# Hybrid conv/RWKV-7 block: the last LayerNorm in the first phase, BK times KR in quarters, squares in two parts, and a refitted planner clock

## The chip, the cores and the metric

The kernel runs on one core of a Trainium2 chip. The metric is the device time of one execution in microseconds, median over runs of one program. The engines are TensorE (PE; PEld is its weight load), VectorE (DVE), ScalarE (ACT), GpSimd (POOL) and SyncE (SP, which here issues the transfers).

## The reference

Sequence 2048, width 1024, one layer. The input is normalised and modulated, then projected once to 9344 columns, which feed two branches; both are gated, projected, merged and projected again.

```python
h = _rmsnorm(x, norm_g[l]) * (1.0 + scale[:, None, :]) + shift[:, None, :]
p = jnp.einsum('bsd,de->bse', h, w_in[l])
# conv branch
u = val * jax.nn.sigmoid(gate)
u = _causal_depthwise_conv(u, conv_k, conv_b)      # 31 taps per channel
u = _layernorm(u, ln_g, ln_b, LN_EPS)              # over the 1024 channels
y_conv = (jax.nn.silu(u) * jax.nn.silu(og)) @ w_o
# rwkv branch: token shift, then per head of 64
kk = (k * k_k); kk = kk / max(sqrt(sum(kk * kk)), L2_EPS)
state = state * w_t - (state @ kk_t) (kk_t * a_t) + v_t k_t     # a scan over time
y_rwkv = (groupnorm(o) + bonus) * jax.nn.silu(og) @ w_o
# merge
m = sigmoid(g_conv) * y_conv + sigmoid(g_rwkv) * y_rwkv
x = x + gate * (m @ w_out);  out = _rmsnorm(x, final_g)
```

## The kernel before

**Layout.** Channels lie on partitions, time on the free axis. Time is cut into 4 blocks b of 512 steps (`NB`, `TB`), channels into 8 tiles j of 128 (`KT`). Products in full accuracy are made from two fp32r parts: `hi` is the value cast to fp32r (ACT), `lo` the value minus `hi` (DVE or POOL), and three products hi*hi, hi*lo, lo*hi are summed in PSUM (`mm3k`, L347). A projection is 24 such matmuls of 512 columns.

**First phase** (`manual_schedule`, from L1425). For each block, four groups g of 18 projections each. The projections k, r, vv of the two pairs of a group (a pair q is two heads, 128 channels) feed `pair` (L755); the others are the convolution's gate and value ("c") and the four gates "1" to "4" (`order`, L1358, with the lists `FILL` and, for the last group, `LAST`). Results that are needed later go to DRAM scratch: `y_dram` (after the 31 taps), `co_dram`, `ro_dram`, `gr_dram`, `gc_dram` (gates), `z_dram` (rwkv branch before its projection), `u_dram` (conv branch before its projection). The phase ends with `rows0` (L1456): both branch projections of block 0, "ro" then "co".

**Order by a model clock.** Every engine call goes through `note` (L85), which keeps a modelled time for each engine (`RATE`, constants for SP and PE) and for each tile. Work beside the projections is written as Python generators, `Task`s with a rank (0 first); `poll` (L152) emits their next instructions when the model says that what they wait for (`ok`, `idle`, `room`, `bank`, `burst`) is there. So the constants in `note` decide in which order instructions stand in each engine's queue. On the chip each engine takes its queue in order; an instruction put too early blocks those behind it.

**What the change touches in `pair`.** The squares of k (`sq`, ACT) are summed over the 64 channels of each head by a product with `bones`, a block matrix of ones, in plain fp32 (L806 to L808); the sums go to `ssr` and to DRAM (`G.dN`), where the group's chain reads them. Then `y` and `BK` are made, and L841 to L855 multiply `BK` by `KR` for each chunk of 64 steps: for each head `hh` 64 contraction rows, 128 output partitions, 128 columns, into one of two PSUM banks `pA`; DVE masks the result into `Asb`. One burst is 8 such products (16 records, since fp32 takes two each); a pair has two bursts.

**LayerNorm.** For blocks 0 to 2 it is `lnorm_first` (L1189), part of the side tasks of the next block (`sides`, L1323, rank 3, one after the other, from group 1 on): pass 1 loads the 8 tiles of y and sums them (POOL), a product with `ones` gives the mean; pass 2 loads them again, subtracts, squares (ACT), sums; a second product gives the variance and `rsteps` (L273) the inverse root on DVE in ten steps; pass 3 loads y a third time, subtracts and multiplies on POOL, applies swish (ACT, DVE), multiplies by the gate and stores to `u_dram`. Buffers are `hx` (L503), a ring of 7 tiles shared with the input norm (`xnorm`), the group's end (`zb`, `zr`), `hload` (which fetches the next block's input) and `presplit` (L305). `presplit` writes the hi and lo parts of the 8 `w_ro` and 8 `w_o` tiles to DRAM, in two halves each; `sides` places four in block 1, four in block 2 and eight in block 3.

For block 3 the norm is `lnorm` (L1566) in the second phase, with y kept in 8 tiles of pool `b2` and two PSUM tiles `pmean`, `pvar`.

**Convolution.** `conv` (L1144) makes `u`; `taps` (L1170, rank 4) adds the 31 taps on DVE into a PSUM tile and stores y. There are three `u` tiles, and a `u` waits for the convolution three before it.

**Second phase** (from L1601, ordered by the tile framework's own scheduler). For each block b: `cproj` of the conv branch (b > 0), loads and splits of the next block's z and u (`lsplit`, through 6 `ld` buffers), the output product (`part`, 384 matmuls of 256 columns, PSUM tiles `pout`), the residual sum and squares (`addx`), the final norm (`tail_rs`, `finish`), and `rproj` of the next block, whose results `mr` share buffers with the stored outputs `xt`.

## Time and profile before

| | us |
|---|---|
| median of 3 runs (lowest, highest) | 2893.17 (2893.12, 2894.62) |
| the profiled execution, its own time | 2892.82 |
| its span, first to last instruction | 2890.7 |

The page gives each engine's busy share, 40 slices, and the costliest groups. All rows name L129, the line of the wrapper through which every call goes, so groups are told apart by tile names (`out<-in`). In a timeline row stand start, duration, engine, operation, tiles, shape and count, and in brackets the idle time before it and what ended it. PE durations overlap (matmuls are pipelined): the distance of two starts is what a matmul costs.

### The profile page before, as it was taken

The page shows a single profiled execution, that of the slowest core. Times are in us where ns is not written, and L with a number is a line of the kernel's source. Part 1 is how long each engine was busy: PE and PEld are TensorE (multiplying, and loading weights), DVE is VectorE, ACT ScalarE, POOL GpSimd, SP SyncE. Part 2 cuts the span into 40 slices and gives each one's busy share as a digit, 9 for nine tenths or more (in the row PEclk, how much of TensorE's full clock was granted, in tenths as well). Part 3 has the DMA queues.
Part 4 walks back from the last instruction along what each step waited for, and adds up shares of the span by engine and source line. Part 5 has one row for each costly group of instructions (what it writes and reads, how often), then busy time and mean ns, then how long its engine had stood idle before and what let it go on. Part 6 is the DMA issues. An engine that isn't in the chain of part 4 may idle for free.

```text
span 2890.7 us, 52304 instructions
## 1 busy us (share of the span) xinstructions
PE 2725.4 (94%) x19472; PEld 2201.6 (76%) x19472; DVE 2058.8 (71%) x3575; ACT 1090.7 (38%) x2180; POOL 1257.7 (44%) x1772
## 2 busy tenths in 40 slices
PE   6999999889999999999999999999999998899998
PEld 5777777667777777787777777777777777698988
DVE  6877787869677878885868787669787666543343
ACT  5545344434243434443434443333434233221211
POOL 0564746533528355444656462648373633100000
PEclk9999999989999999999999999999999999999999
DMA  8786767666757566776756686866666848676665
GB/s 329 255 295 219 281 221 263 237 227 234 231 187 257 183 218 237 250 258 221 252 181 233 205 294 201 273 211 215 205 246 213 294 158 314 234 240 229 215 226 175
DMA packets 361742, 680.47 MB, mean 235 GB/s; under 512 B 134160, under 2 KB 152912, under 8 KB 361488
## 3 DMA queue, kind: packets, MB, share of 16 engines
q1 hardware_dynamic: 361488, 677.13, 69.0%
q8 instruction: 154, 2.52, 0.4%
q14 instruction: 100, 0.82, 0.1%
HBM read 494.34 MB, written 181.54 MB: 234 GB/s over the span
## 4 chain that ended last, share of the span: by engine, by line
PE 32%; DVE 9%; POOL 7%; DMA 5%; issue 3%; ACT 1%; SPq 1%; DVEq 0%; POOLq 0%; ACTq 0%
PE ps_main L129 21%; PE pout L129 5%; DVE acc L129 3%; PE xo L129 2%; PE aux L129 2%; POOL TT L129 2%; POOL itmp L129 1%; PE late L129 1%; SPq L129 1%; DVE S L129 1%; DMA w_lo<-kl_in 1%; POOL oc L129 1%; DVE gst L129 1%; DVE rs_t L129 1%; POOL lny L129 1%
## 5 line engine op out<-in xcount | busy, mean ns | idle before, releaser
L129 PE MATMUL ps_main<-h_hi,w_hi 128*128 128x512 f32 x2432 | 1016.7, 418 | 17.4 <-DVE lora L129 4.6
L129 PE MATMUL ps_main<-h_hi,w_lo 128*128 128x512 f32 x2432 | 967.7, 398 | 20.3 <-POOL w_lo L129 13.6
L129 PE MATMUL ps_main<-h_lo,w_hi 128*128 128x512 f32 x2432 | 963.8, 396 | 2.0 <-DVE h_lo L129 2.0
L129 DVE SCALAR_TENSOR_TENSOR acc<-u,ck,acc 128x512 f32<-128x512 f32 x928 | 697.5, 752 | 25.3
L129 PEld LDWEIGHTS ps_main<-h_hi,w_lo 128*128 128x128 f32 x2432 | 463.4, 191 | 130.7 <-POOL w_lo L129 16.8
L129 PEld LDWEIGHTS ps_main<-h_hi,w_hi 128*128 128x128 f32 x2432 | 464.0, 191 | 128.9 <-issue 10.0
L129 PEld LDWEIGHTS ps_main<-h_lo,w_hi 128*128 128x128 f32 x2432 | 464.9, 191 | 99.8 <-issue 7.8
L129 POOL TENSOR_TENSOR w_lo<-w_st,w_hi 128x1024 fp32r<-128x1024 f32 (+1 forms) x83 | 165.2, 1990 | 302.9 <-ACT w_hi L129 248.7
L129 POOL TENSOR_TENSOR TT<-TT,itmp 128x126 f32<-128x126 f32 (+22 forms) x496 | 207.3, 418 | 38.9
L129 ACT ACTIVATE th<-ps_main 128x512 f32<-128x512 f32 x160 | 95.6, 598 | 333.9 <-PE ps_main L129 281.7
L129 ACT CAST w_hi<-w_st 128x1024 fp32r<-128x1024 f32 (+1 forms) x135 | 127.2, 943 | 243.2 <-DMA w_st<-w_co_t 137.3
L129 POOL TENSOR_TENSOR itmp<-La,TT 128x126 f32<-128x126 f32 (+22 forms) x496 | 200.8, 405 | 37.1 <-issue 6.4
L129 DVE SCALAR_TENSOR_TENSOR S<-xo,pe,Se 64x64 f32<-64x64 f32 x512 | 145.0, 283 | 90.1 <-PE xo L129 65.3
L129 ACT COPY uv<-xo 64x256 f32<-64x256 f32 (+1 forms) x192 | 81.0, 438 | 238.3 <-PE xo L129 164.7
L129 POOL TENSOR_TENSOR lny<-lny 128x512 f32<-128x512 f32 x90 | 119.9, 1340 | 108.9 <-DMA lny<-y_d 87.0
L129 DVE TENSOR_TENSOR w_lo<-w_st,w_hi 128x1024 fp32r<-128x1024 f32 x52 | 72.4, 1392 | 68.3 <-PE ps_main L129 46.5
L129 ACT ACTIVATE Se<-S,pe 128x128 f32<-128x128 f32 x256 | 88.7, 396 | 83.2 <-DVE S L129 82.7
L129 DVE TENSOR_TENSOR As<-aux,maskA 128x512 f32<-128x512 f32 x128 | 82.3, 685 | 52.5 <-PE aux L129 52.5
L129 POOL TENSOR_TENSOR wlo<-wf,wl 64x128 fp32r<-64x128 f32 x64 | 31.2, 488 | 149.6 <-ACT wl L129 147.0
L129 ACT ACTIVATE t<-ps_main,mu 128x512 f32<-128x512 f32 x96 | 65.9, 687 | 77.6 <-PE ps_main L129 68.0
L129 DVE TENSOR_TENSOR xt<-pout,xt 128x256 f32<-128x256 f32 x64 | 24.4, 419 | 99.3 <-PE pout L129 93.2
L129 PEld LDWEIGHTS xo<-S,KR 128*128 128x128 f32 x512 | 76.8, 189 | 23.9 <-DVE S L129 5.3
(298 smaller groups left out, 5029.0 us busy)
## 6 DMA issues: line engine op xcount, KB each, us to landing
w_hi<-kh_in SPq DMA_DIRECT2D x219, 512.0 KB
w_lo<-kl_in SPq DMA_DIRECT2D x219, 512.0 KB
w_st<-w_in_t SPq DMA_DIRECT2D x73, 512.0 KB
kh_in<-w_hi SPq DMA_DIRECT2D x71, 512.0 KB
kl_in<-w_lo SPq DMA_DIRECT2D x71, 512.0 KB
lny<-y_d SPq DMA_DIRECT2D x72, 256.0 KB
w_hi<-kh_ro SPq DMA_DIRECT2D x32, 512.0 KB
w_lo<-kl_ro SPq DMA_DIRECT2D x32, 512.0 KB
```

Of the source, the lines that this page charges most:

```text
L129: r = f(*a, **k)
```

## The change

Five edits. (1) `note`: SP 0.45 us instead of 0.36 an issue, ACT 0.1 us more per further operand, scans at twice the rate per element, `scalar_tensor_tensor` of 64 columns 0.08 us more. (2) `sq` is split into two fp32r parts, and two fp32r products replace the plain one. (3) Each product of BK and KR is cut into two of 64 output partitions, so that one burst is 16 products (32 records) of 64x64. (4) `lnorm` and its pools go; `last_norm` runs `lnorm_first` for block 3 as a second task of rank 3, with the adding and multiplying on DVE, once the last convolution is done, in buffers of its own (`Slots`: the three `u` tiles and `yj`, three lent from `hx` after the norm of block 2, three more when the pairs are done). In all four norms, pass 2 squares into a tile of its own and stores y minus mean back to `y_dram`, so that pass 3 subtracts no more. (5) The order around it: block 3 has its convolutions in groups 0 to 2 (`LAST`), the norm of block 2 begins in group 0 of block 3, `presplit`s stand eight in block 1 and eight in block 2, `ld` has 8 buffers, and in the second phase the loads of x come ahead of the split of z, that of u behind the residual sums.

```diff
@@ -42,9 +42,12 @@
 WB = 6
+LDB = 8
+SLACK = 2.0
 KEPT = ("in",)
 FILL = ("c", "1", "3", "4", "2", "c", "1", "3", "4", "2")
-LAST = ("c", "1", "c", "3", "4", "2", "1", "3", "4", "2")
+LAST = ("c0 10 20 c1 21 11 22 c2 23", "c3 12 24 c4 25 13 26 c5 27", "c6 14 30 c7 31 15 32 33 34 35",
+        "16 36 37 40 41 17 42 43 44 45 46 47")
 DMA_RATE = 330e3
@@ -107,12 +110,19 @@
         elif name == "SP":
-            vt["SP"] = t + 0.36
+            vt["SP"] = t + 0.45
             vt["DMA"] = max(vt["DMA"], t) + size(out) * out.shape[0] * 4 / DMA_RATE
             c0, c1_ = RATE[name] if op != "memset" else (0.1, 0.9e-3)
-            end = vt[name] = t + c0 + c1_ * max([size(out)] + [size(a) for a in ins[:1]])
+            n_ = max([size(out)] + [size(a) for a in ins[:1]])
+            if name == "ACT":
+                c0 += 0.1 * max(len(ins) - 1, 0)
+            elif op == "tensor_tensor_scan":
+                c1_ *= 2
+            elif name == "DVE" and op == "scalar_tensor_tensor" and n_ == CH:
+                c0 += 0.08
+            end = vt[name] = t + c0 + c1_ * n_
         ready[k_] = max(ready.get(k_, 0.0), end)
@@ -235,6 +245,25 @@
                 self.free.append(max(ready.get(key(t), 0.0), used.get(key(t), 0.0)))
+
+    class Slots(Ring):
+
+        def room(self, n=1, keep=0):
+            return Ring.room(self, n)
+
+        def __init__(self, slots):
+            self.free, self.slots, self.held = [0.0] * len(slots), list(slots), {}
+
+        def take(self, name):
+            self.free.remove(min(self.free))
+            slot = self.slots.pop(0)
+            t = slot(name)
+            self.held[key(t)] = slot
+            return t
+
+        def give(self, *ts):
+            Ring.give(self, *ts)
+            self.slots.extend(self.held.pop(key(t)) for t in ts)
@@ -803,9 +832,17 @@
                                            scalar=vc("rwkv_k_k", pr), in1=E1x[:, :, e, :], op0=ALU.mult, op1=ALU.mult)
-        yield burst(ok(sq), free, bank("aux"))
+        yield ok(sq)
+        sh = e1.tile([P, TB], F32R, name="sq_hi", tag=RHT)
+        nc.scalar.copy(sh, sq)
+        yield ok(sh)
+        sl = e1.tile([P, TB], F32R, name="sq_lo", tag=YT)
+        dve = max(now[0], vt["POOL"]) > max(now[0], vt["DVE"]) + W2
+        (nc.vector if dve else nc.gpsimd).tensor_tensor(out=sl, in0=sq, in1=sh.bitcast(F32), op=ALU.subtract)
+        yield burst(ok(sl), free, bank("aux"))
         pss = pa.tile([P, TB], F32, name="aux", tag="aux")
-        nc.tensor.matmul(pss, bones.bitcast(F32), sq, start=True, stop=True)
+        nc.tensor.matmul(pss, bones, sh, start=True, stop=False)
+        nc.tensor.matmul(pss, bones, sl, start=False, stop=True)
         ssr = e1.tile([P, TB], F32, name="ssr", tag="sq")
@@ -844,10 +881,12 @@
                 es = slice(e * 128, e * 128 + 128)
-                for hh in range(2):
+                for i in range(4):
+                    hh, half = i % 2, i // 2
                     hs = slice(64 * hh, 64 * hh + 64)
-                    nc.tensor.matmul(pA[hh][:, c // 2, es], BK[hs, cc, es], KR[hs, cc, es],
-                                     start=(c == 0), stop=(c == 3), skip_group_check=True)
+                    rs = slice(64 * half, 64 * half + 64)
+                    nc.tensor.matmul(pA[hh][rs, c // 2, es], BK[hs, cc, e * 128 + 64 * half:e * 128 + 64 * half + 64],
+                                     KR[hs, cc, es], start=(c == 0), stop=(c == 3), skip_group_check=True)
             for hh in range(2):
@@ -1186,13 +1225,16 @@
-    def lnorm_first(b):
+    def lnorm_first(b, hx):
             nc.sync.dma_start(yj, y_dram[b][j])
+            if b + 1 == NB:
+                ready[key(yj)] += SLACK
             return yj
+        eng = nc.vector if b + 1 == NB else nc.gpsimd
         yield hx.room(3, 1)
@@ -1201,7 +1243,7 @@
             yield ok(ys, yj)
-            nc.gpsimd.tensor_tensor(out=ys, in0=ys, in1=yj, op=ALU.add)
+            eng.tensor_tensor(out=ys, in0=ys, in1=yj, op=ALU.add)
             hx.give(yj)
@@ -1216,32 +1258,46 @@
             yield ok(yj, mean)
-            nc.gpsimd.tensor_tensor(out=yj, in0=yj, in1=mean, op=ALU.subtract)
-            yield ok(yj)
-            nc.scalar.activation(yj, yj, AF.Square)
+            eng.tensor_tensor(out=yj, in0=yj, in1=mean, op=ALU.subtract)
+            yield both(ok(yj), hx.room(1))
+            yq = hx.take("lnq")
+            nc.scalar.activation(yq, yj, AF.Square)
+            nc.sync.dma_start(y_dram[b][j], yj)
+            hx.give(yj)
             if j == 0:
-                qs = yj
+                qs = yq
             else:
-                yield ok(yj)
-                nc.gpsimd.tensor_tensor(out=qs, in0=qs, in1=yj, op=ALU.add)
-                hx.give(yj)
+                yield ok(yq)
+                eng.tensor_tensor(out=qs, in0=qs, in1=yq, op=ALU.add)
+                hx.give(yq)
         yield burst(ok(qs), free, bank("late"))
         rl, rt = hx.take("lnr"), hx.take("lnt")
-        for _ in rsteps(rl, qs, rt):
-            yield idle("DVE", 0.3)
-        hx.give(qs, rt)
+        for n, _ in enumerate(rsteps(rl, qs, rt)):
+            if n % 3 == 0:
+                yield idle("DVE", 0.3)
+        hx.give(qs, rt, mean)
+        def both_of(j):
+            yj, ct = yload(j), hx.take("lnc")
+            nc.sync.dma_start(ct, co_dram[b][j])
+            return yj, ct
+
+        nxt = None
         for j in range(KT):
-            yield hx.room(3, 1)
-            yj, ct, th = yload(j), hx.take("lnc"), hx.take("lnth")
-            nc.sync.dma_start(ct, co_dram[b][j])
+            if nxt is None:
+                yield hx.room(3, 1)
+                nxt = both_of(j)
+            else:
+                yield hx.room(1)
+            yj, ct = nxt
+            th, nxt = hx.take("lnth"), None
+            if j + 1 < KT and b + 1 == NB and hx.room(2)() is not None:
+                nxt = both_of(j + 1)
             yield ok(yj, rl)
-            nc.gpsimd.tensor_tensor(out=yj, in0=yj, in1=mean, op=ALU.subtract)
-            yield idle("POOL", 0.3)
-            nc.gpsimd.tensor_tensor(out=yj, in0=yj, in1=rl, op=ALU.mult)
+            eng.tensor_tensor(out=yj, in0=yj, in1=rl, op=ALU.mult)
             yield ok(yj)
@@ -1249,12 +1305,12 @@
             yield ok(yj, ct)
-            nc.gpsimd.tensor_tensor(out=yj, in0=yj, in1=ct, op=ALU.mult)
+            eng.tensor_tensor(out=yj, in0=yj, in1=ct, op=ALU.mult)
             hx.give(ct)
             hx.give(yj)
-        hx.give(mean, rl)
+        hx.give(rl)
@@ -1327,14 +1383,20 @@
             yield from gate_col()
-        if b and g == 1:
-            yield from lnorm_first(b - 1)
+        if b and g == (0 if b + 1 == NB else 1):
+            yield from lnorm_first(b - 1, hx)
+            if b + 1 == NB:
+                yield from lend(3)
         if b:
-            for _ in range((4, 2, 2, 0)[g] if b + 1 == NB else (1, 0, 1, 2)[g]):
+            for _ in range(0 if b + 1 == NB else (1, 1, 3, 3)[g]):
                 n_ = later.pop(0)
+    def slot_of(pool, tag, n):
+        return lambda name: pool.tile([P, TB], F32, name=name, tag=tag, bufs=n)
+
+    more = Slots([slot_of(e2, "u", 3)] * 3 + [slot_of(e2, "yj", 1)])
     reached, normed = [-1], [0]
@@ -1342,6 +1404,17 @@
+    def lend(n):
+        yield hx.room(n)
+        for _ in range(n):
+            more.free.append(min(hx.free))
+            hx.free.remove(min(hx.free))
+            more.slots.append(hx0)
+
+    def last_norm():
+        yield when(lambda: len(convs) == KT * NB and convs[-1].done)
+        yield from lnorm_first(NB - 1, more)
+
     def proj(h, ti, name, box):
@@ -1356,12 +1429,14 @@
     def order(b, g):
-        todo, cj, gj = list(FILL if b + 1 < NB or g < 3 else LAST), [2 * g, 2 * g + 1], {w: [2 * g, 2 * g + 1] for w in "1234"}
+        cj, gj = [2 * g, 2 * g + 1], {w: [2 * g, 2 * g + 1] for w in "1234"}
+        todo = [(w, (cj if w == "c" else gj[w]).pop(0)) for w in FILL]
+        if b + 1 == NB:
+            todo = [(w_[0], int(w_[1])) for w_ in LAST[g].split()]
             for _ in range(n):
-                w = todo.pop(0)
-                yield w, (cj if w == "c" else gj[w]).pop(0)
+                yield todo.pop(0)
@@ -1444,7 +1519,7 @@
         nc.vector.tensor_scalar(out=ck, in0=ck, scalar1=0.5, scalar2=None, op0=ALU.mult)
-        side.append(Task(side_work(), 3))
+        side.extend((Task(side_work(), 3), Task(last_norm(), 3)))
         for b in range(NB):
@@ -1482,6 +1557,8 @@
               enumerate(("M", "ta", "E2", "k", "r", "vv", "y", "sh"))]
+        more.free.extend([0.0] * 3)
+        more.slots.extend(slot_of(e1, t_, 1) for t_ in ("lw", "la", "E1"))
         h = rows0(h, "ro", gr_dram[0], u_dram[0])
@@ -1505,7 +1582,7 @@
     def ldt(name, src):
-        t_ = ob.tile([P, TB], F32, name=name, tag="ld", bufs=6)
+        t_ = ob.tile([P, TB], F32, name=name, tag="ld", bufs=LDB)
         nc.sync.dma_start(t_, src)
@@ -1545,9 +1622,7 @@
-    b2 = ctx.enter_context(tc.tile_pool(name="b2", bufs=2, reuse_waits="tile"))
     hl = ctx.enter_context(tc.tile_pool(name="hl", bufs=1, reuse_waits="tile"))
-    pa = ctx.enter_context(tc.tile_pool(name="pa2", bufs=1, space=PSUM, reuse_waits="tile"))
     po = ctx.enter_context(tc.tile_pool(name="po2", bufs=4, space=PSUM, reuse_waits="tile"))
@@ -1555,56 +1630,14 @@
     fg = f2.tile([P, D], F32, name="fg", tag="fg", bufs=1)
-    nc.sync.dma_start(fg, final_g.unsqueeze(0).broadcast_to([P, D]))
-    def t2(name):
-        return b2.tile([P, TB], F32, name=name, tag="t2", bufs=3)
-
     def utiles():
         return [uhi[:, j, :] for j in range(KT)], [ulo[:, j, :] for j in range(KT)]
-
-    def lnorm(b):
...
-        return uhi, ulo
             cproj(b, uhl, (mhi, mlo))
-        if b + 1 < NB:
-            ohl = lsplit(z_dram[b + 1], okt(b + 1))
-            uhl = lsplit(u_dram[b + 1], utiles()) if b + 2 < NB else lnorm(b + 1)
         xts = []
@@ -1614,6 +1647,10 @@
             xts.append(xh)
+        if b + 1 < NB:
+            ohl = lsplit(z_dram[b + 1], okt(b + 1))
+        if b == 0:
+            nc.sync.dma_start(fg, final_g.unsqueeze(0).broadcast_to([P, D]))
         sq4 = f2.tile([P, NTT, 4], F32, name="sq4", tag="sq4")
@@ -1672,6 +1709,7 @@
         if b + 1 < NB:
+            uhl = lsplit(u_dram[b + 1], utiles())
             rall = tail_rs(0, NTT)
                 finish(tt, rall)
```

31 lines of the change are left out of this document (removed).

## The prediction

> **What bounds the kernel now.** I read the page first (busy shares, then the 40 slices), then what TensorE waited for, then PE's busy time by stretch, and last the PE timeline at the places that the change touches.
>
> ```profile
> PE 2725.4 (94%) x19472; PEld 2201.6 (76%) x19472; DVE 2058.8 (71%) x3575; ACT 1090.7 (38%) x2180; POOL 1257.7 (44%) x1772
> PE   6999999889999999999999999999999998899998
> ```
>
> TensorE is busy 94% of the span, and the slices dip at three places only: the start, one slice near 610 us, and two near the border of the phases. So time goes down in two ways: less PE work, or less PE waiting. The stretches (us; busy us of PE, PEld, DVE, ACT, POOL with instruction counts; clock; DMA share; GB/s) say where the waiting is, and the waits of PE say for what:
>
> ```profile
> 0.00:2290.00 2290.00, 2167.99 (x15959) 1715.82 (x15960) 1767.07 (x3070) 943.69 (x1872) 1187.17 (x1717) 0.99 0.70 238
> 2397.20:2890.00 492.80, 455.05 (x2694) 404.26 (x2692) 225.57 (x393) 118.59 (x255) 36.58 (x24) 0.97 0.68 234
> ```
> ```profile
> PE ps_x L129 <- DMA w_st<-w_in_t: 15.3, 1, 15.3
> PE ps_main L129 <- DVE mr L129: 14.2, 2, 12.8
> PE ps_main L129 <- POOL w_lo L129: 13.6, 6, 4.8
> PE aux L129 <- ACT sq L129: 13.4, 12, 2.6
> PE pout L129 <- DVE o_lo L129: 2.6, 3, 1.1
> ```
>
> Up to 2290 us PE is idle 2290 - 2168 = 122 us, spread over many short waits. From 2397 us on it is idle 493 - 455 = 38 us, in few places, and the change removes what stands there.
>
> **Squares in two parts.** Each of the 32 pairs (8 pairs in each of 4 blocks) puts one plain fp32 product of `bones` and `sq` between projection matmuls:
>
> ```profile
> 122.12 0.40 PE L129 MATMUL ps_main<-h_hi,w_lo 128*128 128x512 f32 x1
> 122.36 1.02 PE L129 MATMUL aux<-sq,bones 128*128 128x512 f32 x2
> 122.81 0.80 PE L129 MATMUL ps_main<-h_hi,w_hi 128*128 128x512 f32 x1
> 123.45 0.39 PE L129 MATMUL ps_main<-h_lo,w_hi 128*128 128x512 f32 x1
> ```
> ```profile
> 244.80 0.39 PE L129 MATMUL aux<-la,wl 128*128 128x512 f32 x1
> 245.03 0.39 PE L129 MATMUL aux<-la,wlo 128*128 128x512 f32 x1
> 245.26 0.39 PE L129 MATMUL ps_main<-h_hi,w_hi 128*128 128x512 f32 x1
> ```
>
> The second fence has products of the kind that takes its place (fp32r, 512 columns): start to start 0.23 us, as a projection matmul. In the first fence 1.33 us lie between 122.12 and 123.45, of which two projections are 0.46: the plain product costs 0.87 us, two of the new ones 0.46. Saved: 0.41 x 32 = 13.1 us. The operands cost an ACT copy (0.62 us, the row of `rh` below) and a subtraction on POOL (1.28, the row of `s_lo`) or DVE, 32 times. ACT at 38% and POOL at 44% hide them; the pair's chain gets some 2 us longer, behind which `ssr`, `y` and `BK` of that pair queue. PE waits for it only if the planner (the model clock that orders the instructions) puts the product too early, as it did 12 times for 13.4 us; bounds of that wait are 0 and twice 13.4, and I leave it unchanged.
>
> ```profile
> L129 ACT CAST rh<-rk x32: 617/619/623, 92.5 to 2243.9; 128x512 fp32r<-128x512 f32 x32
> L129 POOL TENSOR_TENSOR s_lo<-rk,rh x32: 1262/1284/2267, 93.5 to 2246.3; 128x512 fp32r<-128x512 f32 x32
> L129 DVE SCALAR_TENSOR_TENSOR rk<-r,hrk,ta x32: 740/1484/2929, 91.3 to 2242.5; 128x512 f32<-128x512 f32 x32
> ```
>
> **BK times KR in quarters.** The work is the same, in 64x64 tiles four abreast instead of 64x128 tiles two abreast:
>
> ```profile
> 133.98 0.39 PE L129 MATMUL ps_main<-h_hi,w_lo 128*128 128x512 f32 x1
> 134.30 1.16 PE L129 MATMUL aux<-KR,BK 64*128 64x128 f32 x16
> 135.39 0.51 PE L129 MATMUL ps_main<-h_hi,w_hi 128*128 128x512 f32 x1
> ```
> ```profile
> 1355.51 0.27 PE L129 MATMUL late<-As,Tn 64*64 64x64 f32 x1
> ...
> 1355.97 0.23 PE L129 MATMUL aux<-As,Tn 64*64 64x64 f32 x2
> 1356.03 0.22 PE L129 MATMUL aux<-As,Tn 64*64 64x64 f32 x2
> ```
>
> A burst of 16 records lasts 135.39 - 134.30 = 1.09 us now. The group's chain already runs 64x64 tiles four abreast into the same two banks: four records each 0.058 us (1355.97 to 1356.03) at 64 columns, so about 0.117 at 128. Eight such sets are 0.94, and with a start and a switch as now about 1.06. I take -2 us over the 64 bursts. Bounds: -4, and +57 if the two column halves run one after the other (eight more steps of about 0.11 us, 0.89 x 64).
>
> **The last LayerNorm leaves the second phase.** The same 384 output matmuls of the first and the third block (rows of `pout`, PE, PEld and DVE), and PE's waits beside them:
>
> ```profile
> 2397.20:2462.80 65.60, 49.80 (x384) 48.01 (x384) 5.36 (x14) 0.92 0.89 329
> 2701.20:2746.50 45.30, 45.25 (x384) 45.20 (x384) 5.29 (x14) 1.00 0.58 204
> ```
> ```profile
> 2419.02 2.07 PE L129 MATMUL pmean<-ys,ones 128*128 128x512 f32 x2 [6.28 <-POOL ys L129]
> 2430.18 0.38 PE L129 MATMUL pout<-w_lo,o_hi 128*128 128x256 f32 x1 [1.76 <-DMA w_lo<-kl_o]
> 2438.17 0.58 PE L129 MATMUL pout<-w_hi,o_hi 128*128 128x256 f32 x1 [2.49 <-DVE xt L129]
> 2486.74 0.80 PE L129 MATMUL ps_main<-m_hi,w_hi 128*128 128x512 f32 x1 [12.81 <-DVE mr L129]
> 2624.60 0.51 PE L129 MATMUL ps_main<-o_hi,w_hi 128*128 128x512 f32 x1 [1.35 <-DVE mr L129]
> ```
>
> The first block takes 65.6 us where an undisturbed one takes 45.3: 20.3 us lost to `pmean` standing in PE's queue, to DVE and DMA shared with the norm, and to a clock of 0.92. Right after it comes a wait of 12.81 us for `mr`, which stands on DVE behind the norm's rsqrt and products. Without the norm, about 3 us stay at the start (the split of `mr` itself, by the waits for `o_lo`: 2.6 us), and of the 12.81 about 1.35 stays, since `mr` shares its buffer with the stored output, as the next block shows. Saved: 17.3 + 11.5 + some 0.6 of slow clock = 29.4 us. The two products with `ones` move into the first phase, at 0.87 us each by the `sq` row: +1.7. Net -27.7; bounds -20 (half of the 20.3 stays, its DMA share of 0.89 now made by `u` and `z`) and -32. The splits of `u`, now behind the sums of each block, are 8 DVE steps (0.74 us each) beside 90 us of matmuls in which DVE is half idle; uncovered they push `finish` and with it `mr`, 5.9 us in each of three blocks.
>
> **The norm's own cost where it goes.** It starts when the 32nd convolution is done and needs three more buffers, which come after the side tasks' norm of block 2 or when the pairs are done. Side tasks run one after another:
>
> ```profile
> L129 SPq DMA_DIRECT2D kl_o<-w_lo x8: 319/334/755, 1754.5 to 1891.4; - x8
> L129 SPq DMA_DIRECT2D lny<-y_d x24: 342/426/1366, 1891.7 to 2128.9; - x24
> L129 SPq DMA_DIRECT2D u_d<-lny x8: 319/320/486, 2030.6 to 2176.0; - x8
> L129 SPq DMA_DIRECT2D u_d<-lny x8: 320/320/385, 1501.1 to 1654.4; - x8
> L129 SPq DMA_DIRECT2D kl_ro<-w_lo x6: 319/319/320, 1204.3 to 1252.1; - x6
> L129 POOL TENSOR_TENSOR lny<-lny 128x512 f32<-128x512 f32 x90 | 119.9, 1340 | 108.9 <-DMA lny<-y_d 87.0
> ```
>
> One half of a `w_o` split takes 137/7 = 19.6 us, one of a `w_ro` split (1252 - 1204)/5, some 10. The norm of block 1 ended at 1654; three more `w_ro` splits and one of `w_o` now stand ahead of it (6 x 10 + 2 x 19.6 = 99 us), and each early norm loses 8 POOL subtractions of 1.34 us and a pause, some 14 us: two norms, so 1725. Fourteen halves of `w_o` follow: 2000. The norm of block 2 took 2176 - 1892 = 284 us, now 270: it ends near 2270, 94 us later than before. PE leaves the first phase at 2397 - 15 = 2382. The last norm has its sums done by then; for the rest the bounds are its bare DVE work (57 steps less the 7 sums, at 0.74 us the best `rk`: 37 us) and the 284 us of block 2's norm. It loads ahead and shares its buffers with nobody, so I take 100, nearer the low end: 2370, in time by 12 us. If that cover is gone, DVE and SP work through the rest ahead of the first splits, and PE stands for as long. On SP its 48 transfers take about 0.43 us each to issue (median of the `lny<-y_d` row), 20 us over some 200, ahead of the weight loads queued behind them. The eight new `y_d` stores of each of the four norms are 256 KB each, 8 MB in all; eight splits of 1.5 MB leave block 3.
>
> On DVE the convolutions crowd into block 3's first three groups:
>
> ```profile
> 1722.00:2148.00 426.00, 408.85 (x3067) 323.53 (x3067) 319.12 (x540) 162.06 (x324) 237.68 (x342) 0.99 0.69 230
> 1722.00:2148.00 426.00, 142.99 (x191) 0.99 0.69 230
> ```
>
> DVE is busy 319 of 426 us, 143 of them taps (the second row is `acc` alone). Eight convolutions instead of six are some 43 us more: 362, 85%. PE's waits on DVE there should grow; I take +4 (0 to +15). The refitted clock (ACT +0.1 us per operand, scans twice, SP 0.45 us) changes every order in the first phase: of 122 us idle I take -3, bounds -20 and +20.
>
> The Trainium skill, SBUF — State Buffer, section "Who interferes with whom", speaks against moving this work to DVE: with two inputs in SBUF it contends with a GpSimd instruction that reads SBUF, and the later one blocks fully. The `rk` row agrees (740 ns at best, 1484 median); by it the norm's 57 DVE steps would take nearer 1.48 than 0.74 us, up to 42 us more of DVE time; if half of it fell behind the pairs' end, that would turn the 12 us in hand into some 9 us late, which is rival (a) at its mild end.
>
> **Sum.** -13.1 - 2 - 27.7 + 4 - 3 = -41.8 us. The profiled execution took 2892.8 us (span 2890.7 and 2.1 around it), 0.4 under the median of the runs: 2892.8 - 41.8 = 2851.
>
> **Rivals.**
> (a) *The last norm ends late.* For it: 12 us in hand after a chain of estimates, and a far bound 270 us late. Against it: PE's order gives DVE much room after the convolutions, and three buffers come at the end of the pairs anyway. Ten to 40 us late, middle 25: 2876. Only from 42 us late on would the kernel be slower than before.
> (b) *The quarters do not run four abreast* at 128 columns. Place: the 64 bursts; price +57; it decides alone, since 57 is over 42: from 0.65 us per burst on, the kernel is slower. 2851 + 2 + 57 = 2910. Against it stand the 0.058 us sets of the chain.
> (c) *The new order waits more in the first phase*: crowded DVE, later parts of squares, `w_lo` from a POOL that runs the splits in blocks 1 and 2. A quarter more idle than 122 us is +30: 2881. For it: a wait moved is often a wait elsewhere; against: POOL loses the eight subtractions of each of the three early norms.
>
> **How the numbers follow.** Forecast 0.60, (a) 0.25, (b) 0.05, (c) 0.10. A measurement of this kernel tells 0.2%, 5.8 us, from no change. Faster: the forecast whole, most of (a) and of (c): 0.90; same 0.03; slower 0.07, from (b) and the worst of (a). The range reaches from 2832 (all gains at their bounds, waits 15 us less) to 2880, which takes in (a) and most of (c).
>
> **What would show it.** Right: `aux<-sq` gone and two fp32r products 0.23 us apart; bursts of 32 records in about 1.06 us; the first block's 384 `pout` matmuls in under 50 us and no wait over 3 us before `rproj`; the last `u_d` store before PE's first `pout`; PE idle near 120 us in the first phase. Wrong: stores of `u_d` after the first `pout` with PE standing, bursts near 2 us, or a first phase shortened by less than 8 us.

## The result, and the profile after

| | before | after |
|---|---|---|
| median of runs taken together, us | 2893.89 (4 runs, 2893.12 to 2896.97) | 2914.90 (4 runs, 2911.85 to 2919.05) |
| ratio, 95% interval | | 1.0078 [1.0059, 1.0097] |
| profiled execution: own time, span | 2892.82, 2890.7 | 2911.85, 2910.1 |

The changed kernel is 0.8% slower; 2851 was forecast. The page after has the same rows as before; all of them now name L139:

```profile
PE 2707.0 (93%) x20496; PEld 2196.6 (75%) x20496; DVE 2069.0 (71%) x3611; ACT 1112.8 (38%) x2213; POOL 1222.2 (42%) x1744
PE   6999899999999989999999999998999995999998
PEclk9999999999999999999999999999999997999999
```

PE is busy 18 us less than before (2707.0 against 2725.4), in a span 19 us longer. One slice is down to 5, at the border of the phases, and the granted clock falls there too. The view by stretches, cut at the end of the first phase's last matmul and at the first `pout`, splits the difference (columns as before: length; busy us with counts of PE, PEld, DVE, ACT, POOL; clock, DMA share, GB/s). Before:

```profile
0.00:2397.40 2397.40, 2270.56 (x16782) 1797.52 (x16782) 1833.21 (x3182) 972.06 (x1925) 1221.13 (x1748) 0.98 0.70 236
2397.40:2890.70 493.30, 454.85 (x2693) 404.10 (x2691) 225.57 (x393) 118.59 (x255) 36.58 (x24) 0.97 0.68 234
```

After:

```profile
0.00:2409.80 2409.80, 2256.72 (x17808) 1794.20 (x17808) 1872.19 (x3238) 1001.46 (x1971) 1219.65 (x1742) 0.98 0.71 240
2409.80:2442.40 32.60, 0.00 (x0) 0.00 (x0) 16.78 (x25) 13.66 (x20) 2.52 (x2) 0.55 0.86 315
2442.40:2488.40 46.00, 45.99 (x385) 46.00 (x386) 17.93 (x36) 18.10 (x49) 0.00 (x0) 0.95 0.82 304
2442.40:2910.10 467.70, 450.33 (x2688) 402.38 (x2688) 180.02 (x349) 97.67 (x223) 0.00 (x0) 0.98 0.66 231
```

First phase +12.4 (2409.8 - 2397.4), border +32.6, second phase -25.6 (467.7 - 493.3): +19.4, the difference of the spans. In the first phase PE's busy time fell by 13.8 (2270.56 to 2256.72), and its idle time, which is length less busy time, rose from 126.8 to 153.1. The waits of PE after (us in total, times, longest):

```profile
PE pout L139 <- ACT o_hi L139: 32.6, 1, 32.6
PE aux L139 <- POOL KR L139: 23.3, 15, 4.2
PE aux L139 <- DVE sq_lo L139: 2.3, 3, 1.2
PE aux L139 <- POOL sq_lo L139: 1.4, 3, 0.7
PE ps_main L139 <- DVE mr L139: 6.9, 3, 3.6
```

The wait for the squares, 13.4 us before (`aux` for `sq`), is down to 3.7 (the two rows of `sq_lo`); that for `KR` is up from 10.2 to 23.3.

The 32.6 us at the border have their story in the timeline (start, duration, engine, operation):

```profile
2243.73 0.32 SPq L139 DMA_DIRECT2D y_d<-yj  x1
2249.46 1.49 DVE L139 TENSOR_TENSOR lny<-lny 128x512 f32<-128x512 f32 x1
...
2289.99 0.82 DVE L139 TENSOR_TENSOR lny<-lny 128x512 f32<-128x512 f32 x1
...
2365.16 0.69 DVE L139 TENSOR_SCALAR lnq<-late 128x512 f32<-128x512 f32 x1
...
2385.27 2.85 POOL L139 TENSOR_TENSOR w_lo<-w_st,w_hi 128x1024 fp32r<-128x1024 f32 x1
2385.89 2.78 DVE L139 SCALAR_TENSOR_TENSOR lnr<-lnt,lnr 128x512 f32<-128x512 f32 x1
...
2400.16 0.32 SPq L139 DMA_DIRECT2D u_d<-lny  x1
...
2435.89 0.40 SPq L139 DMA_DIRECT2D u_d<-lny  x1
...
2439.21 2.62 ACT L139 CAST m_hi<-zt 128x512 fp32r<-128x512 f32 x4 [0.57 <-DMA zt<-z_d]
2441.74 4.26 ACT L139 CAST o_hi<-mr 128x512 fp32r<-128x512 f32 x8
2442.41 0.58 PE L139 MATMUL pout<-w_hi,o_hi 128*128 128x256 f32 x1 [32.64 <-ACT o_hi L139]
```

The last convolution is stored at 2243.7; the last norm adds its eight tiles until 2290.8, its squares until 2365, its rsqrt until 2388.7, and stores `u` from 2400 to 2436. The second phase's first work stands behind it in the queues, and on ACT eight casts of z stand ahead of the first `o_hi` as well.

The products came out as the prediction said:

```profile
126.42 0.39 PE L139 MATMUL ps_main<-h_hi,w_lo 128*128 128x512 f32 x1
126.65 0.40 PE L139 MATMUL aux<-sq_hi,bones 128*128 128x512 f32 x1
126.88 0.40 PE L139 MATMUL aux<-sq_lo,bones 128*128 128x512 f32 x1
127.12 0.40 PE L139 MATMUL ps_main<-h_hi,w_hi 128*128 128x512 f32 x1
...
137.64 1.10 PE L139 MATMUL aux<-KR,BK 64*64 64x128 f32 x32
138.68 0.50 PE L139 MATMUL ps_main<-h_hi,w_hi 128*128 128x512 f32 x1
```

The products of the squares start 0.23 us apart, and 32 records of quarters take 1.04 us from start to the next start: they run four abreast.

### The profile page after: what moved, and what is told of

Same layout as the page of the kernel before. It is cut to its first block, busy times and chain, and to the rows that moved or that the text cites. A ratio compares the mean times of both kernels' runs of the same rounds, so it can differ in the third digit from the quotient of the medians.

```text
span 2910.1 us, 54492 instructions
## 1 busy us (share of the span) xinstructions
PE 2707.0 (93%) x20496; PEld 2196.6 (75%) x20496; DVE 2069.0 (71%) x3611; ACT 1112.8 (38%) x2213; POOL 1222.2 (42%) x1744
## 4 chain that ended last, share of the span: by engine, by line
PE 42%; POOL 11%; DMA 10%; DVE 7%; issue 3%; SPq 2%; ACT 1%; DVEq 0%; POOLq 0%; ACTq 0%
PE ps_main L139 27%; PE pout L139 6%; PE xo L139 4%; POOL TT L139 3%; POOL itmp L139 3%; PE aux L139 3%; DVE acc L139 2%; PE late L139 2%; SPq L139 2%; POOL lny L139 2%; DMA As<-dT 1%; DMA hf<-xT 1%; POOL oc L139 1%; DVE S L139 1%; DMA w_lo<-kl_in 1%
## 5 line engine op out<-in xcount | busy, mean ns | idle before, releaser
L139 PE MATMUL ps_main<-h_hi,w_hi 128*128 128x512 f32 x2432 | 1005.5, 413 | 20.4 <-DVE k L139 6.7
L139 PE MATMUL ps_main<-h_hi,w_lo 128*128 128x512 f32 x2432 | 968.2, 398 | 19.9 <-POOL w_lo L139 13.8
L139 PE MATMUL ps_main<-h_lo,w_hi 128*128 128x512 f32 x2432 | 964.9, 397 | 3.6 <-issue 2.7
L139 DVE SCALAR_TENSOR_TENSOR acc<-u,ck,acc 128x512 f32<-128x512 f32 x928 | 698.4, 753 | 29.3 <-POOL u L139 3.8
L139 PEld LDWEIGHTS ps_main<-h_hi,w_lo 128*128 128x128 f32 x2432 | 463.8, 191 | 132.0 <-POOL w_lo L139 16.4
L139 PEld LDWEIGHTS ps_main<-h_hi,w_hi 128*128 128x128 f32 x2432 | 465.3, 191 | 129.3 <-issue 13.7
L139 PEld LDWEIGHTS ps_main<-h_lo,w_hi 128*128 128x128 f32 x2432 | 465.9, 192 | 92.3 <-DVE h_lo L139 2.7
L139 POOL TENSOR_TENSOR w_lo<-w_st,w_hi 128x1024 fp32r<-128x1024 f32 (+1 forms) x86 | 173.1, 2012 | 316.8 <-ACT w_hi L139 272.4
L139 POOL TENSOR_TENSOR TT<-TT,itmp 128x126 f32<-128x126 f32 (+22 forms) x496 | 211.9, 427 | 38.9
L139 POOL TENSOR_TENSOR itmp<-La,TT 128x126 f32<-128x126 f32 (+22 forms) x496 | 205.2, 414 | 39.4 <-issue 9.4
L139 ACT CAST w_hi<-w_st 128x1024 fp32r<-128x1024 f32 (+1 forms) x135 | 127.6, 946 | 239.9 <-DMA w_st<-w_co_t 105.9
L139 DVE SCALAR_TENSOR_TENSOR S<-xo,pe,Se 64x64 f32<-64x64 f32 x512 | 145.0, 283 | 96.7 <-PE xo L139 69.6
L139 ACT ACTIVATE th<-ps_main 128x512 f32<-128x512 f32 x160 | 95.5, 597 | 267.8 <-PE ps_main L139 218.2
L139 ACT COPY uv<-xo 64x256 f32<-64x256 f32 (+1 forms) x192 | 81.2, 439 | 255.4 <-PE xo L139 185.3
L139 DVE TENSOR_TENSOR w_lo<-w_st,w_hi 128x1024 fp32r<-128x1024 f32 x49 | 66.3, 1353 | 67.3 <-PE ps_main L139 50.6
L139 DVE TENSOR_TENSOR As<-aux,maskA 128x512 f32<-128x512 f32 x128 | 82.4, 686 | 41.7 <-PE aux L139 40.8
L139 ACT ACTIVATE Se<-S,pe 128x128 f32<-128x128 f32 x256 | 88.9, 396 | 51.8 <-DVE S L139 50.9
L139 DVE TENSOR_TENSOR xt<-pout,xt 128x256 f32<-128x256 f32 x64 | 24.4, 420 | 109.7 <-PE pout L139 109.7
L139 PE MATMUL pout<-w_hi,o_hi 128*128 128x256 f32 x256 | 71.8, 284 | 32.6 <-ACT o_hi L139 32.6
L139 PE MATMUL aux<-KR,BK 64*64 64x128 f32 x2048 | 75.9, 281 | 27.9 <-POOL KR L139 23.3
L139 ACT ACTIVATE t<-ps_main,mu 128x512 f32<-128x512 f32 x96 | 66.0, 687 | 84.5 <-PE ps_main L139 76.5
L139 PEld LDWEIGHTS aux<-KR,BK 64*64 64x64 f32 x2048 | 58.4, 136 | 50.7 <-POOL KR L139 30.1
```

Source lines behind the costliest of these rows:

```text
L139: r = f(*a, **k)
```

## The experiments

Three questions: what the border's wait is, whose the new idle time in the first phase is, and what the second phase's gain is worth without the wait before it. In the table the first phase ends with its last matmul, idle is that stretch less PE's busy time in it, and the rest is span less first phase. These three are from one profiled execution each, which can lie up to 12 us from the median (e7: 2910.35 against 2922.59); the ratio is against the kernel before on the same chip.

| run | median us | ratio [95%] | first phase | idle | rest |
|---|---|---|---|---|---|
| before | 2893.89 | | 2397.4 | 126.8 | 493.3 |
| after | 2914.90 | 1.0078 [1.0059, 1.0097] | 2409.8 | 153.1 | 500.3 |
| e1 after, old clock | 2903.34 | 1.0047 [1.0030, 1.0065] | 2430.9 | 155.9 | 473.4 |
| e2 after, KR in halves | 2924.35 | 1.0123 [1.0108, 1.0138] | 2445.4 | 181.0 | 477.5 |
| e3 before, squares in two parts | 2903.43 | 1.0049 [1.0031, 1.0067] | 2408.0 | 151.1 | 491.8 |
| e4 after, norm in second phase | 2898.15 | 1.0030 [1.0014, 1.0045] | 2399.6 | 144.8 | 496.9 |
| e5 before, SP 0.37 | 2888.76 | 0.9996 [0.9977, 1.0016] | 2398.7 | 132.4 | 489.2 |
| e6 before, SP 0.35 | 2909.45 | 1.0062 [1.0040, 1.0084] | 2410.6 | 143.1 | 492.6 |
| e7 after, SP 0.46 | 2922.59 | 1.0104 [1.0063, 1.0145] | 2432.5 | 177.3 | 476.1 |
| e8 after, short norm | 2897.97 | 1.0028 [1.0010, 1.0046] | 2410.2 | 151.8 | 488.8 |
| e9 e3 with SP 0.37 | 2932.24 | 1.0133 [1.0112, 1.0154] | 2424.4 | 159.0 | 500.5 |
| e10 before, quarters | 2912.86 | 1.0067 [1.0045, 1.0089] | 2421.7 | 146.7 | 489.9 |
| e11 e8, old clock, z by POOL | 2903.90 | 1.0038 [1.0022, 1.0054] | 2419.6 | 153.7 | 472.2 |
| e12 e11, KR in halves | 2921.01 | 1.0094 [1.0073, 1.0116] | 2432.0 | 161.1 | 481.3 |
| e13 before, squares in one part | 2904.44 | 1.0059 [1.0036, 1.0082] | 2410.4 | 153.0 | 490.0 |
| e14 e3, subtraction on DVE | 2937.70 | 1.0181 [1.0160, 1.0202] | 2424.6 | 160.8 | 511.8 |
| e15 before, norm moved | 2891.90 | 1.0022 [1.0007, 1.0038] | 2416.0 | 144.0 | 471.9 |
| e16 e15 with SP 0.35 | 2889.34 | 1.0002 [0.9986, 1.0019] | 2405.0 | 139.9 | 476.6 |
| e17 before, norm held back | 2884.56 | 0.9974 [0.9956, 0.9992] | 2403.8 | 133.2 | 484.7 |
| e18 before, refitted clock | 2884.79 | 0.9980 [0.9963, 0.9996] | 2371.9 | 115.5 | 509.5 |

e17 leaves the first phase's instructions as they were: 2403.8 against 2397.4 is what two executions of one order differ by.

**Each part undone.** The clock's numbers, the quarters, and the norm's place, each taken back in the changed kernel; e4 puts block 3's `lnorm` and its pools back into the second phase, behind the splits of z, with six `ld` buffers again.

```diff
-            vt["SP"] = t + 0.45
+            vt["SP"] = t + 0.36
```
```diff
-        side.extend((Task(side_work(), 3), Task(last_norm(), 3)))
+        side.append(Task(side_work(), 3))
...
+            if b + 2 == NB:
+                uhl = lnorm(b + 1)
```

> The changed kernel, with the operation times of the trace order's clock as they were before (SP 0.36 us, no 0.1 us per ACT operand, scans and the 64-column scalar_tensor_tensor as other DVE steps). Theory C (the refitted clock makes the worse order: it costs most of the 26.4 us of new PE idle time in the first phase and pushes the last norm late): 2914.9 goes to about 2860 (PE idle of the first phase back near 127 us, and the 32.6 us wait of pout for o_hi gone or under 10 us). Theory Q (the quarters, which the clock prices at 1.88 us a burst for 1.09 real ones, make the worse order): 2905 to 2920, and the wait for o_hi stays over 20 us. Theory N (any new order moves the first phase by some 10 us either way, and the last norm is too long by itself): 2895 to 2925, o_hi wait 20 to 45 us.

> The changed kernel, with BK times KR as 8 products of 64x128 again. Theory Q (the clock's too high price of the quarters sets PE ahead of the plan; KR waits 23.3 us instead of 10.2): KR waits back to some 10 us and first phase 10 to 26 us shorter, 2889 to 2905, the o_hi wait the same or shorter. Theory C (refitted clock): no gain, 2910 to 2920, KR waits near 23 us. By the bursts alone (1.30 us inserted either way) nothing changes.

> The changed kernel, with block 3's LayerNorm in the second phase again, computed there from the stored y, beside the first output block; LAST, the splits of weights, the quarters, the squares and the refitted clock stay as changed. If the last norm's lateness costs the 32.6 us wait and its absence from the second phase gives 25.8 us, then 2914.9 - 32.6 + 25.8 = 2908, and the idle time of blocks 0 to 2 stays at 113 us (51.9 + 33.5 + 27.6). If instead the crowded norm is what slows block 3 and rows0 (their idle 40.2 against 28.8 before), 2897. Far under 2890 would say that the second phase did not lose by the norm at all.

e1: the border's wait went (0.7 us) and the first phase became 21 us longer; none of the three theories had both. Its PE busy time rose as well (2430.9 - 155.9 = 2275.0 against 2256.7, with the same 17808 records), so the busy time of one order is no exact measure of work. e2 went the wrong way, by 36 us of first phase, for a part whose bursts cost the same, though the waits for `KR` fell (16.9); its wait at the border fell to 1.4 too. e4 came out at the second of its three values, near 2897: without the last norm the first phase is 10 us shorter.

**Squares alone, and their forms.**

> The kernel before, with the squares in two parts alone. By the prediction's term -13.1 us: 2880.8. If the new order waits where the saved time was (theory N), between 2880 and 2900, with the net cost of an insertion still down from 0.88 to 0.47 us and PE idle in the first phase up by as much.

> The kernel before with the squares in two parts, and SP's issue at 0.37 instead of 0.36 us (the step that left the kernel before at 2888.8). If the loss of the squares alone (first phase 2408.0, PE idle 151.1 us, the waits for POOL 59.7 us up to 2395 us against 33 to 38 in three orders without them) belongs to the squares (theory S: the subtraction on POOL, and a chain 2 us longer, push KR and what stands behind it on POOL), idle stays over 145 us and the waits for POOL over 50, time 2896 to 2910. If it was a draw (theory N), idle falls to 125 to 140, the waits for POOL to 33 to 45, and the time to 2878 to 2890, 13 us of PE work under the kernel before.

```diff
-        dve = max(now[0], vt["POOL"]) > max(now[0], vt["DVE"]) + W2
-        (nc.vector if dve else nc.gpsimd).tensor_tensor(out=sl, in0=sq, in1=sh.bitcast(F32), op=ALU.subtract)
+        nc.vector.tensor_tensor(out=sl, in0=sq, in1=sh.bitcast(F32), op=ALU.subtract)
```

> The kernel before with the squares in two parts and every subtraction on DVE. If it is the 15 subtractions on POOL (19.5 us of POOL work) that delay KR, the waits for POOL fall from 60 to 35 to 45 us and idle to 130 to 145, in part made up by waits for DVE (45 to 55). If it is the longer chain, or the saved PE time, the waits for POOL stay over 50. The end of the first phase may carry a late norm of block 2 beside this.

```diff
-        sq = e1.tile([P, TB], F32, name="sq", tag="sq")
+        sq = e1.tile([P, TB], F32R, name="sq", tag="sq")
...
-        nc.tensor.matmul(pss, bones.bitcast(F32), sq, start=True, stop=True)
+        nc.tensor.matmul(pss, bones, sq, start=True, stop=True)
```

> The kernel before with the squares rounded to fp32r as ACT writes them, and one product of bones: the low part of the squares is left out, and with it the copy and the subtraction. PE work falls by (0.87 - 0.23) x 32 = 20 us. Theory S (the subtraction on POOL and the longer chain cost the waits): the waits for POOL up to 2395 us stay at 33 to 40, PE idle of the first phase 120 to 140, time 2865 to 2880. Theory P (the saved PE time returns as waiting, since what surrounds PE sets the pace): idle 145 to 165, time 2885 to 2900.

The kernel with the squares alone was slower than before in both orders, in e3 by no more than a step of the order alone costs (e6, below). In e3 PE's busy time fell by 13.7 (2270.6 to 2408.0 - 151.1 = 2256.9), and idle rose by 24.3. In e9, set against e5 with the same SP number, busy time stayed (2265.4 and 2266.3) and idle rose by 26.6. Of the losses of e9 and e14, some 17 us are a wait of `pout` for `o_hi` at the border (16.9 and 16.7). The waits for `KR`, before and in e3, up to 2395 us:

```profile
PE aux L129 <- POOL KR L129: 10.2, 10, 2.1
```
```profile
PE aux L129 <- POOL KR L129: 29.1, 16, 7.7
```

The longest of them in e3 shows how a queue passes a delay on:

```profile
775.57 0.62 ACT L129 CAST w_hi<-w_st 128x512 fp32r<-128x512 f32 x1 [11.48 <-DMA w_st<-w_ro_t]
776.26 1.27 POOL L129 TENSOR_TENSOR w_lo<-w_st,w_hi 128x512 fp32r<-128x512 f32 x1 [5.14 <-ACT w_hi L129]
777.49 1.17 POOL L129 TENSOR_TENSOR KR<-r,E 128x512 f32<-128x512 f32 x1
778.71 2.08 PE L129 MATMUL aux<-KR,BK 64*128 64x128 f32 x16 [7.67 <-POOL KR L129]
```

ACT waited for a weight load of a side task, POOL's split waited for ACT, `KR` stood behind that split without a wait of its own, and PE waited for `KR`. Such waits for POOL, summed over all rows up to 2395 us, are 43.5 to 65.0 us in the eleven runs with squares in two parts (e14 61.2, so it is not the subtraction's engine) and 31.9 to 40.4 in the nine without (e13 31.9). Those for `KR` alone overlap: 16.9 to 32.1 in the eleven, 9.6 to 18.7 in the nine. Against them stands the wait for the squares themselves, which the two parts shorten: 13.4 us before, 4.1 in e3, 6.8 in e14. What the two parts lengthen is the chain from `sq` to `KR`. One pair of the kernel before, and one after, both near the median of their 32:

```profile
1533.17 0.72 ACT L129 ACTIVATE sq<-k,v 128x512 f32<-128x512 f32 x1
1535.11 0.59 ACT L129 COPY ssr<-aux 128x512 f32<-128x512 f32 x1 [0.63 <-PE aux L129]
1543.58 1.64 POOL L129 TENSOR_TENSOR KR<-r,E 128x512 f32<-128x512 f32 x1
```
```profile
1455.73 0.72 ACT L139 ACTIVATE sq<-k,v 128x512 f32<-128x512 f32 x1
1461.02 0.59 ACT L139 COPY ssr<-aux 128x512 f32<-128x512 f32 x1 [3.92 <-PE aux L139]
1469.91 1.18 POOL L139 TENSOR_TENSOR KR<-r,E 128x512 f32<-128x512 f32 x1
```

From the end of `sq` to the end of `ssr` it is 1.8 us before and 5.2 after; to the end of `KR` it is 11.3 and 14.6. So theory S fits the waits for POOL, by the longer chain. But e13, which has neither copy nor subtraction and products 20 us cheaper, has a first phase of 2410.4 all the same. Three rows of its waits, up to 2395 us, have grown instead:

```profile
PE ps_main L129 <- ACT w_hi L129: 12.7, 3, 7.7
PE ps_main L129 <- DVE w_lo L129: 10.1, 6, 4.5
PE ps_main L129 <- DVE vv L129: 7.0, 2, 3.7
```

They are 4.1, 4.7 and nothing in the kernel before: waits for weights and projections, as theory P has it. In no order tried did cheaper squares by themselves shorten the first phase: 2408.0, 2424.4, 2424.6 and 2410.4, though the first and the last are no longer than e6's 2410.6, which has the old squares.

**Steps that change nothing but the order.** One number of the clock is moved by 0.01 us, in both kernels.

> The kernel before with one number of the clock changed, SP's time of an issue 0.37 instead of 0.36 us. No operation is added or removed; only the places of some instructions in the queues move. Theory N (the old order was a favourable draw among many of its kind; any step out of it costs PE idle time of the first phase, whatever the step): PE idle of the first phase goes from 126.8 to 140 to 155 us, the time to 2900 to 2915. Theory S (the new waits belong to the squares in two parts, as in the run of the squares alone: 151.1 us idle): idle 120 to 133, time 2885 to 2897.

> As the run before it, with 0.35 us. Theory N: idle 140 to 155 us, 2900 to 2915; theory S: idle 120 to 133, 2885 to 2897. If one of the two moves up and the other stays, the spread of orders is as large as the steps of the change, and the old order is not special.

> The changed kernel with SP's issue at 0.46 instead of 0.45 us. Theory N for the changed kernel too: the first phase (2409.8) moves by 10 us or more either way, and the wait for o_hi (32.6) by as much the other way or the same; 2900 to 2940. Theory S: 2910 to 2920, and the first phase within 3 us of 2410.

In the kernel before one step did nothing and the other cost 0.6%; in the changed kernel the first phase became 22.7 us longer and the border's wait fell to 1.4 (476.1 of rest). So a single order of a part says its worth to some 20 us only.

**Quarters alone, and the refitted clock alone.**

> The kernel before with BK times KR in quarters alone. By the bursts (1.30 us inserted either way): no change, 2889. Theory Q (priced at 1.88 us a burst for 1.09 real ones, PE runs ahead of the plan by some 23 us over the 64 bursts and waits for what the plan thinks done): PE idle 126.8 goes to 140 to 155 us and the time to 2900 to 2915.

> The kernel before with the refitted clock alone (SP 0.45 us, ACT operands, scans, 64-column steps). By the prediction's term: -3 us with bounds of 20 either way, 2886. If every new order of the first phase costs what the null steps and the parts cost (phase 1 of 2399 to 2424 against 2397), 2890 to 2920. A late norm of block 2 at the border may come beside it.

e10 is 24 us longer in the first phase and lies in theory Q's ranges; e2, where the quarters are taken back, says the opposite by 36. What the quarters do to the order is not told from an order's own spread, and theory Q is not settled. e18 surprised: the first phase falls to 2371.9, the shortest of all, by 11.3 us of idle and 14.1 of busy time with the same products, and the border and the block behind it take most of that back.

```profile
0.00:2371.90 2371.90, 2256.42 (x16780) 1789.45 (x16780) 1823.69 (x3182) 968.60 (x1918) 1207.03 (x1738) 0.99 0.70 236
2371.90:2387.40 15.50, 0.06 (x2) 0.06 (x1) 0.07 (x1) 2.54 (x5) 9.99 (x9) 0.50 1.02 353
```
```profile
PE ps_main L136 <- DVE mr L136: 20.5, 4, 17.9
PE pout L136 <- ACT o_hi L136: 15.4, 1, 15.4
```

At the border POOL is busy for 10 of 15.5 us and PE has nothing to do.

**The last norm made short.** The tiles are added as the convolutions end, loads run three ahead, rsqrt goes in two lots, and the last pass in two lanes:

```diff
-        yield when(lambda: len(convs) == KT * NB and convs[-1].done)
-        yield from lnorm_first(NB - 1, more)
+        yield from lnorm_last(NB - 1, more)
...
+        for j in range(1, KT):
+            yield conved(j)
...
+        lanes = [Task(lane(), 3) for _ in range(NL)]
```

> The changed kernel with its last norm written to be short: the sum of y is taken tile by tile as the convolutions end, three loads run ahead in the second pass, the ten rsqrt steps go in two lots, and the last pass runs in two lanes. Theory T (the 32.6 us wait of pout for o_hi is the norm's lateness and nothing else): the wait falls under 10 us and the time to 2880 to 2892. Rival: the time comes back as PE idle in rows0, since the norm's DVE steps then stand before the evacuations of mr: wait gone, rows0 10 to 25 us longer, 2898 to 2912.

> The changed kernel with the short last norm, the old constants of the clock, and the last group's two stores of z issued by POOL, behind the POOL product they wait for, instead of SP. In the run of the short norm SP stood until 2423 for such a store with the loads of xt behind it, and PE 13.5 us for xt. If that store is the next wait, no wait of pout is over 6 us and the second phase takes 470 to 478 us instead of 487.4. With a first phase of 2400 to 2431 (as the draws so far) 2875 to 2905. If the second phase's start is bound by its own loads instead, pout still waits 8 to 14 us and the second phase takes 480 to 490.

> As the run before it, with BK times KR as 8 products again. By the bursts alone the same time; by theory Q a first phase 10 to 25 us shorter than in the run before it, 2865 to 2890.

In e8 the border's wait is 1.4 us, the first phase is as in the changed kernel (2410.2), and the ratio falls from 1.0078 to 1.0028, some 14 us. The rest of the 32.6 came back, most of it as a wait that no theory had named. The rows of e8's timeline and of its waits:

```profile
2412.71 0.32 SPq L140 DMA_DIRECT2D z_d<-oc  x1
...
2422.07 1.29 POOL L140 TENSOR_TENSOR oc<-oc,zr 128x512 f32<-128x512 f32 x1
2423.39 0.32 SPq L140 DMA_DIRECT2D z_d<-oc  x1
...
2425.20 4.00 SPq L140 DMA_DIRECT2D xt<-x_in  x8
```
```profile
PE pout L140 <- DVE xt L140: 14.3, 2, 13.5
```

SP stood for the last group's z, with the loads of `xt` behind it. With that store on POOL (e11) the wait for `xt` is gone, and the rest is 472.2; but 10.8 us of it are a wait at the border, over the 6 expected, for casts of z that stand ahead of `o_hi` on ACT and wait for their loads. e12, expected faster than e11, was slower.

**The move alone, and the norm held back in its old place.** e15 and e16 have the fast norm, z by POOL and the first splits ahead, and the old squares, halves and clock.

> The kernel before with the last norm in the first phase alone (with what goes with it: order of the last block, weight splits in blocks 1 and 2, stored differences, the second phase's order), the short form of the last norm, the last stores of z by POOL, and the first splits of the second phase ahead of others. Squares, BK times KR and the clock as before. If the move is worth what the second phase gained (25 us, less what the border takes): first phase 2395 to 2412, border under 5 us, second phase 465 to 475, time 2865 to 2885, under both kernels. If the first phase gives it back (DVE in block 3 and rows0): first phase over 2415, time 2885 to 2900.

> As the run before it, with SP's issue at 0.35 instead of 0.36 us: another order of the same kernel. Theory N: within 15 us of it, either way. If both lie under 2885, the move pays whatever the order.

```diff
+        nc.gpsimd.tensor_copy(ys[:, 0:1], rall[:, 0:1])
         for j in range(KT):
             yj = b2.tile([P, TB], F32, name=f"y{j}", tag=f"y{j}", bufs=1)
+            nc.gpsimd.tensor_copy(yj[:, 0:1], rall[:, 0:1])
             nc.sync.dma_start(yj, y_dram[b][j])
```

> The kernel before, with its last norm held back in the second phase: nine copies of one column from the second block's row factors into the norm's buffers, ahead of its loads, make it wait for them. The first phase's order is untouched. If the second phase lost its time to the norm's early place (6.3 us for ys, 12.8 us for mr, the first block's slow start), the second phase goes from 493.4 to 466 to 476 us, the first stays at 2395 to 2400, and the time falls by 17 to 27 us, to 2862 to 2873, under both kernels. Rival: the norm's steps on DVE delay mr or the sums of a later block by as much (a wait of pout or ps_main over 8 us after 2600), and the time stays within 5 us of before.

With the move the rest is 16.7 to 21.4 us shorter (476.6 and 471.9 against 493.3) and the first phase 7.6 to 18.6 longer: by the two ratios no gain. e17 leaves the first phase alone and saves 8.6 in the second, half or less of what was expected. The first block's 384 output matmuls tell why, in e17 and in e16:

```profile
2403.80:2463.00 59.20, 49.84 (x389) 48.52 (x388) 27.58 (x47) 24.06 (x58) 3.34 (x2) 0.94 0.90 333
```
```profile
2405.00:2459.10 54.10, 47.40 (x384) 46.56 (x385) 24.81 (x45) 24.19 (x58) 0.93 (x2) 0.94 0.96 355
```

There is no norm beside it, and yet it takes 54 to 59 us, with DMA busy 90 to 96%: this block waits for its loads (PE 6.6 us for `xt` in e17, 5.2 in e16). Only behind a hole, a stretch at the border in which PE has nothing to do, is it 45 or 46 us long, as in the changed kernel (46.0 behind 32.6) and in e15:

```profile
2416.00:2425.80 9.80, 0.06 (x1) 0.07 (x1) 1.98 (x3) 1.25 (x3) 1.34 (x2) 0.63 0.86 322
2425.80:2470.80 45.00, 45.00 (x385) 45.00 (x386) 22.26 (x43) 22.00 (x56) 0.00 (x0) 0.97 0.93 346
```

The sum, 9.8 + 45.0, is e16's 54.1 again. e17 and e18 lie just under both kernels; what they give together was not tried.

## Why the prediction was wrong

The forecast was 2851, and the profiled execution took 61 us more. The wait at the border is 32.6 of them. Some 25 are idle time in the first phase: 26.3 more, where the sum had +4 and -3. Some 4 are the second phase, which gained 25.6 for 29.4. Two steps failed: the last norm was to be in time, and the waits of the first phase were to stay. The first is shown; the second is measured, but its cause is open.

**Squares, -13.1: the product was right, the cover was not.** The new products start 0.23 us apart, as forecast. PE's busy time fell by 13.8 with them, but it moves as much between orders of one kernel (18.3 up in e1, 14.1 down in e18). The step that failed is "ACT at 38% and POOL at 44% hide them", with the wait left unchanged: a busy share says nothing of a chain. The wait that the prediction named fell, from 13.4 to 3.7 us. The one that it did not name, for `KR` at the end of a chain 3.3 us longer (it had said 2), rose from 10.2 to 23.3. The first phase was longer in four orders of four, with 24 to 34 us more idle. In the three with two parts the waits for POOL are part of that. Why it is so even without copy and subtraction (e13) is not shown; that the other engines and the loads set the pace there agrees with it.

**Quarters, -2: right as a burst.** A burst takes 1.04 us to the next start, for 1.06 forecast; what the quarters do to the order (+24 in e10, -36 by e2) is open.

**The norm leaves the second phase, -27.7.** Inside the changed kernel it measured -25.6, but that is not its worth. The 20.3 us of the first block were put down to the norm, and 9 to 14 of them are the block's own loads: without norm and without a hole it takes 54 us (e1, e16) or 59 (e17) against the 45.3 of an undisturbed block, and behind a hole 45. The wait for `mr` fell from 14.2 to 6.9, by 7.3 where 11.5 was forecast. Without a hole the rest of e1, e2, e7 and e16 is 15.8 to 19.9 us shorter than before, and that is the term; the price of its going into the first phase is about 10 by one order (e4: 2399.6 against 2409.8), less than an order moves.

**The last norm, "in time by 12 us": late by 32.6.** The start was nearly right by luck, sums at 2290.8 for 2270. The norm of block 2, which was to end at 2270 and set that time, ended at 2147.6; it was the last convolution, stored at 2243.7, that the last norm waited for. The rest was taken as 100 us and took 145, to 2436, since every pass is a string of waits (load, DVE, ACT, DVE) in queues shared with PE's evacuations. Set against 2370 that is 66 late; PE left 28 later than 2382; 12 - 66 + 28 = -26, and the casts of z make it 32.6. All but seven of the norm's 57 DVE steps took about 0.69 us, as bare as the low bound had them. The seven ran beside a POOL instruction and took 0.8 to 2.8 us, some 9 us more in sum. So the rule of the Trainium skill (SBUF — State Buffer, "Who interferes with whom") shows in the trace but did not decide it: 9 us of 145, and POOL had 2.5 us of work in those 32.6. e8, where the short norm leaves 1.4 us of the wait, shows that the norm's lateness was its cause.

**The refitted clock, -3, bounds -20 and +20: right by its bounds.** The term was for idle time, and alone (e18) it is -11.3, with -14.1 of busy time beside it; by the ratio of 0.9980 some 6 us are left of both. In the changed kernel undoing it lengthened the first phase too: 21.1 in e1, and 9.4 from e8 to e11, which has its z stores on POOL besides.

**The rivals were not alternatives.** (a), a late norm, and (c), more waiting in the first phase, each had a price that left the kernel faster, and a chance of its own. They lie in different stretches and both came: 2851 + 32.6 + 25.3 (idle 126.8 to 153.1, less the 1 already in the sum) = 2909 against 2911.85. Slower needed just this sum, and the prediction priced it nowhere. The two are not independent either: in e1, e2 and e7 the first phase was 21 to 36 us longer still, and the wait at the border all but vanished.

## What to carry to other kernels

Rivals that sit in different stretches add up: price them together before giving a chance to "slower". Where one list orders all queues, take the spread of orders first (a step of 0.01 us in one number moved this kernel by 0.6%), and read no part's worth below it from one order. A stage that starts behind a hole hides its loads in it, so its gain has to be read with the hole counted in.

## What the runs showed of the hardware

Four tiles of 64x64 abreast take nearly the time of two of 64x128: 32 records of the one in 1.04 us to the next start, 16 of the other in 1.09 before, at 128 columns. In the stretches in which PE had nothing to do, the granted clock of the row was 0.50 to 0.63 (15.5, 32.6 and 9.8 us long), and 0.95 to 0.97 in the stretches behind them. Seven of the last norm's DVE steps with two inputs began during a POOL instruction, and each ended 0.54 to 0.56 us behind its end: the 2.78 us step at 2385.89 ended at 2388.67, POOL's instruction at 2388.12. The norm's other steps took about 0.69 us.
